# The largest expert moves from the second place to the last, and the final norm runs beside it

## The chip, the core and the metric

The kernel runs on one core of a Trainium2 chip. A core has a matrix engine (PE, with its weight loads shown apart as PEld), a vector engine (DVE), a scalar engine (ACT), GpSimd (POOL) and a synchronisation engine (SP); each works through its own list of instructions in order, and waits on semaphores of the others. 16 DMA engines move data; here SP issues the loads of weights, and POOL the DMAs with indices and those of the final norm. The metric is the time of one execution on the device, in microseconds (us), and the median of several runs is given.

## What is computed

One layer of a hybrid backbone over 1024 latent tokens of 1024 channels: token mixers (spatial gating and bidirectional linear attention), then a mixture of 16 experts of which each token takes two, then a final RMS norm. All values are float32. What matters here is the end:

```python
tokens = (rms_norm(x, g_norm2[layer]) * (1.0 + sc2) + sh2).reshape(-1, d)
...
y = moe_ffn(tokens, w_router, b_router, w_exp_gate[layer], w_exp_up[layer], w_exp_down[layer])
x = x + gt2 * y[:n_lat].reshape(bsz, seq, d)
...
return rms_norm(x, g_final)

def rms_norm(x, g):
    xf = x.astype(jnp.float32)
    y = xf * lax.rsqrt(jnp.mean(xf * xf, axis=-1, keepdims=True) + EPS)
    return (y * g.astype(jnp.float32)).astype(x.dtype)

def expert_block(args):
    xb, e = args
    return (jax.nn.silu(xb @ w_g[e]) * (xb @ w_u[e])) @ w_d[e]
```

With 16 experts and two for each token an expert has 128 tokens on average, some more, some fewer.

## The kernel before

Up to the router the kernel handles mixers and the second norm; the rows after the mixers lie in DRAM as `x1_d`, the normed ones as `h2_d`. Then comes the expert stage, a loop over 16 **slots** (`for e in range(E)`, L1570). `places()` (L1311) ranks the experts by their token counts on the chip, and the table `RANK` (L53) says which rank is worked on in which slot: slot 0 always takes expert 0, slot 1 the rank 1 (the most tokens among the others), slot 15 the rank 15 (the fewest). `UNITS` (L54) follows from it: a slot handles 128 tokens, and besides two, one or no **32-row blocks** for experts with more tokens (two for rank 1, one for ranks 2 to 9, none for the others).

An expert's weights are 18 **pages** of 1 MB: 12 for gate and up (`w_gu`, three thirds of four pages, index `c`), six for down (`w_d`). `load()` (L1175) issues a page on SP into one of ten buffers, in the order of the program, and SP waits there until the buffer is free. Only the 128-row product needs a page split into two parts: `part()` (L1187) makes the high part on ACT (L1192) and the low part on DVE (L1193), into one of three buffers `hl`:

```python
hl = split_tile()
SC.activation(hl[:, 0, :], raw, AF.Copy)
V.tensor_sub(hl[:, 1, :], raw, hl[:, 0, :].bitcast(F32))
```

`block_a` (L1366) multiplies the 128 rows by such a split page, in 12 matmuls of 512 columns. `block_b` (L1376) multiplies the 32-row blocks by the page as it was loaded: the four column quarters of a block stand in the four 32-row strips of the PE's output. In each third a slot with blocks does `block_b` for all four pages first, then `turned_a` (L1557), which transposes the activations of the third before, then `block_a` for the four pages. Behind each third come SiLU on ACT (`sa`, `sb_`) and the product with the up part on DVE. In the down part the pages go in two groups of three, in the same manner. A slot ends with the gate products on DVE, `yb` (L1625) for the blocks and `ya` (L1632) for the 128 rows, and with `put` (L1429): POOL adds the rows into `x1_d` by an indirect DMA that accumulates.

The **final norm** runs beside the last slot. `fetched(i)` (L1507) loads rows 256 i to 256 i + 255 of `x1_d` (block i, 0 to 3) by POOL; it has to wait until the adds of slot 14 have landed. Block 0 has a buffer of its own, the others take page buffers in their turn. `normed(i)` (L1512) squares both halves of the block on ACT (`fq`), makes 1/rms in 12 small steps on DVE (`rstd`, L212), scales by it and by the gain `gf`, and writes to `out` by POOL. `NE` (L48) says for each half who scales: "V" is one DVE operation (L1524), "S" is ACT and then a multiplication on POOL (L1521, L1522). `TAIL` (L49) says behind which third or pair of down pages each step stands in the program (`tail`, L1540). The rows of the last slot's own expert are gathered (`xg`), get `ya` added on the chip, are normed there and scattered over `out` (`put_out`, L1533).

The order on each engine is not that of the program: a scheduler lists each engine's instructions ahead of time, and may put a later step of the program ahead of an earlier one where its data come sooner by its reckoning. If experts overflow their slots, a branch at the end (L1653) repeats work; it is not taken here.

Of the kernel before, what the change touches and what calls it, by code (L numbers as in the profile page):

```python
# [18 lines left out]
S = 1024  # L19
# [25 lines left out]
FQB = 1  # L45
EPX = 1
FOLD = 2
NE = ["SS", "SV", "SV", "VV"]  # L48
TAIL = dict(g0=["f0", "f1"], g2=["g", "n0", "n1", "f2"], d0=["f3"], d2=["n2", "n3"])  # L49
QW = 260  # L50


RANK = (0, 1, 10, 2, 11, 3, 12, 4, 13, 5, 14, 6, 7, 8, 9, 15)  # L53
UNITS = tuple(0 if r == 0 else 2 if r == 1 else 1 if r < 10 else 0 for r in RANK)  # L54
C_C, C_CC, C_G1, C_BB, C_BM, C_GLA, C_LNG = 0, 8, 16, 24, 40, 56, 64
N_COLS = 72
# [105 lines left out]
def body(tc, A, out):  # L162
# [1104 lines left out]
    def pt(name, tag, bufs):  # L1267
        return ps.tile([128, 512], F32, name=name, tag=tag, bufs=bufs)
# [42 lines left out]
    def places():  # L1311

        X = mybir.AxisListType.X
        sq = [128, 16, 16]
        key = ep_.tile([128, 16], F32, name="key")
        V.scalar_tensor_tensor(key, cf, 16.0, ks[:, 3], op0=ALU.mult, op1=ALU.add)
        w = ep_.tile(sq, F32, name="w16")
        V.tensor_tensor(w, key[:, None, :].to_broadcast(sq), key[:, :, None].to_broadcast(sq), op=ALU.is_gt)
        rank = ep_.tile([128, 16], F32, name="rank")
        V.tensor_reduce(rank, w, axis=X, op=ALU.add)  # L1320
        sel = ep_.tile(sq, F32, name="sel")
        V.tensor_tensor(sel, ks[:, 0, :, None].to_broadcast(sq), rank[:, None, :].to_broadcast(sq), op=ALU.is_equal)
        f = ep_.tile([128, 5, 16], F32, name="fi")
        V.tensor_copy(f[:, 0:3], ids)
        V.tensor_scalar(f[:, 3], ks[:, 3], -1.0, 15.0, op0=ALU.mult, op1=ALU.add)
        V.memset(f[:, 3, 0:1], 0.0)
        V.tensor_copy(f[:, 4], cf)
        o = ep_.tile([128, 5, 16], F32, name="fo")
        for i in (3, 0, 1, 2, 4):
            V.tensor_tensor(w, sel, f[:, i, None, :].to_broadcast(sq), op=ALU.mult)  # L1330
            V.tensor_reduce(o[:, i], w, axis=X, op=ALU.add)
            if i == 3:
                V.tensor_mul(key[0:1], o[0:1, 3], ks[0:1, 2])
                V.tensor_reduce(rank[0:1, 0:3], key[0:1, 1:16].rearrange("o (a b) -> o a b", b=5), axis=X, op=ALU.add)
                V.tensor_copy(cnt[:, 0:3], rank[0:1, 0:3])
                words.extend(SP.value_load(cnt[0:1, k:k + 1], min_val=0, max_val=0xFFFFF) for k in range(3))
        V.tensor_copy(ids, o[:, 0:3])
        V.tensor_scalar(tks, ids, 1, None, op0=ALU.logical_shift_right)
        V.tensor_scalar(tkB, tkB, 4, quarter, op0=ALU.mult, op1=ALU.add)
        V.tensor_scalar(chs, ids, 1, None, op0=ALU.bitwise_and)  # L1340

        for b in range(7):
            V.scalar_tensor_tensor(more[:, b], o[0:1, 4], -128.0 * b, ks[0:1, 1], op0=ALU.add, op1=ALU.is_gt)
        V.tensor_copy(more[:, 7], o[0:1, 3])
        V.tensor_copy(more[:, 8], ks[0:1, 1])
        V.tensor_reduce(rank[0:1, 0:1], more[:, 0], axis=X, op=ALU.max)
        V.tensor_copy(cnt[:, 3:4], rank[0:1, 0:1])
# [164 lines left out]
    def normed(i, gf):  # L1512
# [4 lines left out]
            SC.activation(sq, x1[:, j], AF.Square, accum_out=ss[:, 0, j:j + 1])  # L1517
        rstd(ss[:, 1], ss[:, 0], 2, 1.0 / D, ep_)
        for j in range(2):
            if NE[i][j] == "S":  # L1520
                SC.activation(x1[:, j], x1[:, j], AF.Copy, scale=ss[:, 1, j:j + 1])  # L1521
                GP.tensor_mul(x1[:, j], x1[:, j], gf)  # L1522
            else:
                V.scalar_tensor_tensor(x1[:, j], x1[:, j], ss[:, 1, j:j + 1], gf, op0=ALU.mult, op1=ALU.mult)  # L1524
        GP.dma_start(rows_of(out, i), x1)

    def quarters(r0, tile_):
# [10 lines left out]
        return st  # L1538

    def tail(at):  # L1540
        nonlocal gf, xg
        for n in TAIL.get(at, ()):
            if n == "g":
                gf = ep_.tile([128, D], F32, name="gf")
                bcast("rows", 2 * D, D, gf)
                xg = ep_.tile([128, D], F32, name="xg", tag="xa", bufs=1)
                gather(xg, x1_d, tkA[:, E - 1:E])
            elif n[0] == "f":
                fetched(int(n[1]))
            else:  # L1550
                normed(int(n[1]), gf)

    gf = xg = None
    wAB = prep_a(0, *first_xa, ch0), []
    before = []

# [13 lines left out]
    for e in range(E):  # L1570
# [50 lines left out]
        yb = ep_.tile([128, 2, 256], F32, name="yb", bufs=2)  # L1621
        last = e + 1 == E
        wA, wB = wAB_
        for j in range(U):
            V.scalar_tensor_tensor(yb[:, j], pb[:, 256 * j:256 * j + 256], wB[j], g2B, op0=ALU.mult, op1=ALU.mult)  # L1625
        if last:

            sl = ep_.tile([128, 8], F32, name="sl")
            sq = ep_.tile([128, D], BF16, name="fq", bufs=FQB)
        for h in range(2):  # L1630
            hs = slice(512 * h, 512 * h + 512)
            V.scalar_tensor_tensor(ya[:, hs], pa[h], wA, g2A[:, h, :], op0=ALU.mult, op1=ALU.mult)  # L1632
# [3 lines left out]
        if last:  # L1636
            V.tensor_add(sl[:, 6:7], sl[:, 4:5], sl[:, 5:6])
            rstd(sl[:, 7:8], sl[:, 6:7], 1, 1.0 / D, ep_)
            V.scalar_tensor_tensor(xg, xg, sl[:, 7:8], gf, op0=ALU.mult, op1=ALU.mult)
            put_out(xg, tkA[:, e:e + 1], out, S - 1)  # L1640
        if last:
            break
        st = [put(ya, tkA[:, e:e + 1], x1_d, (), before)]
# [9 lines left out]
    any_more = nc.values_load(cnt[0:1, 3:4], min_val=0, max_val=1)  # L1653
    with tc.If(any_more > 0):
        put(ya, tkA[:, E - 1:E], x1_d)
        flat = more.rearrange("o b e -> o (b e)")
        with tc.For_i(0, E, 1) as e:
            with tc.For_i(0, 7, 1) as b:
# [28 lines left out]
```

## Time and profile before

| | |
|---|---|
| time, median of three runs | 2250.44 us (lowest 2249.14 us) |
| the profiled execution: its time | 2251.51 us |
| its span, first to last instruction | 2249.8 us |
| PE busy | 2170.6 us, 96% |
| DVE, ACT, POOL busy | 1415.1, 1056.9, 213.0 us |
| mean granted TensorE clock | 0.984 of 2.4 GHz |

Times of the profile are counted from the start of the span. Lines named L... are those of the kernel before. In a timeline each row is one instruction or a run of like ones; idle time in brackets stands before the row's start. In a table by windows, busy times of PE and PEld overlap. Instructions that only wait or issue a load on SP are not counted as busy.

### The profile page before, as it was taken

To read this page: it belongs to the slowest core of one execution; us is meant where nothing else is said; L and a number is where in the kernel's file an instruction comes from. 1 tells how busy PE (TensorE), PEld (TensorE's weight loads), DVE (VectorE), ACT (ScalarE), POOL (GpSimd) and SP (SyncE) were. 2 spreads that over 40 slices of the span, in tenths; PEclk is the share of its full clock that TensorE was granted. 3 is DMA by queue.
4 is the path that set the end of the run, shared out by engine and by line. 5 is a ranking of instruction groups with operands and counts; after the bars stand their busy time and mean duration, and the time that the engine had idled before them with its cause. 6 is when DMAs were issued, how large, how long until landed. Compare 5 with 4: busy or idle time off the path is not lost. (4 is left out here: it accounts for less than half of the span.)

```text
span 2249.8 us, 36046 instructions
## 1 busy us (share of the span) xinstructions
PE 2170.6 (96%) x14286; PEld 1787.4 (79%) x14287; DVE 1415.1 (63%) x2127; ACT 1056.9 (47%) x1327; POOL 213.0 (9%) x174
## 2 busy tenths in 40 slices
PE   8999999999999999999969999999999999999975
PEld 6999898888889978888967777777778777777754
DVE  5744215847672354245888578787878787677666
ACT  3412114634542244233226456665667576555553
POOL 0011000000000000000342110000101010100031
PEclk9999999999999999999989999999999999999987
DMA  7576433556652176445658779797989898877774
GB/s 295 178 228 177 155 130 102 192 172 208 215 187 71 57 260 208 168 149 195 189 189 319 253 274 362 284 369 297 367 291 377 298 351 314 296 274 284 280 245 157
DMA packets 141792, 529.63 MB, mean 235 GB/s; under 512 B 17127, under 2 KB 57759, under 8 KB 94513
## 3 DMA queue, kind: packets, MB, share of 16 engines
q1 hardware_dynamic: 119584, 467.84, 57.1%
q0 software_dynamic: 20880, 55.16, 8.5%
q10 hardware_dynamic: 1152, 4.26, 0.6%
q8 instruction: 114, 1.87, 0.3%
q14 instruction: 62, 0.50, 0.1%
HBM read 457.09 MB, written 70.31 MB: 234 GB/s over the span
## 5 line engine op out<-in xcount | busy, mean ns | idle before, releaser
L1193 DVE TENSOR_TENSOR hl<-praw,hl 128x2048 fp32r<-128x2048 f32 x174 | 400.2, 2302 | 137.3 <-ACT hl L1192 134.1
L1372 PE MATMUL pa<-hl,xah 128*128 128x512 f32 x1536 | 428.1, 399 | 19.8 <-ACT hl L1192 13.2
L1192 ACT ACTIVATE hl<-praw 128x2048 fp32r<-128x2048 f32 x174 | 333.4, 1918 | 157.8 <-PE pa L1372 150.9
L1372 PEld LDWEIGHTS pa<-hl,xah 128*128 128x128 f32 x1536 | 286.9, 189 | 91.4 <-ACT hl L1192 13.7
L1193 DVE TENSOR_TENSOR hl<-raw,hl 128x2048 fp32r<-128x2048 f32 x114 | 260.7, 2290 | 91.0 <-ACT hl L1192 88.2
L1192 ACT ACTIVATE hl<-raw 128x2048 fp32r<-128x2048 f32 x114 | 218.6, 1918 | 104.0 <-PE pa L1372 98.2
L1372 PE MATMUL pa<-hl,xal 128*128 128x512 f32 x768 | 241.8, 396 | 0.0
L1372 PE MATMUL pa<-hl,aah 128*128 128x512 f32 x768 | 214.8, 401 | 6.3 <-DVE hl L1193 5.0
L256 PE MATMUL mm<-wh,hxh 128*128 128x256 f32 (+1 forms) x768 | 218.2, 284 | 0.9 <-DVE vv L285 0.6
L256 PE MATMUL mm<-wl,hxh 128*128 128x256 f32 (+1 forms) x768 | 216.8, 282 | 0.0
L256 PE MATMUL mm<-wh,hxl 128*128 128x256 f32 (+1 forms) x768 | 216.6, 282 | 0.0
L256 PE MATMUL mm<-hxh,wh 128*128 128x512 f32 x448 | 178.4, 398 | 0.0
L256 PE MATMUL mm<-hxh,wl 128*128 128x512 f32 x448 | 178.2, 398 | 0.0
L256 PE MATMUL mm<-hxl,wh 128*128 128x512 f32 x448 | 178.1, 398 | 0.0
L1372 PEld LDWEIGHTS pa<-hl,xal 128*128 128x128 f32 x768 | 145.5, 189 | 34.0
L1372 PEld LDWEIGHTS pa<-hl,aah 128*128 128x128 f32 x768 | 142.7, 190 | 37.3 <-DVE hl L1193 5.5
L256 PEld LDWEIGHTS mm<-wh,hxh 128*128 128x128 f32 x768 | 144.6, 188 | 1.9 <-DVE vv L285 0.8
L238 DVE TENSOR_TENSOR wl<-wraw,wh 128x2048 fp32r<-128x2048 f32 (+1 forms) x36 | 82.7, 2298 | 99.7 <-ACT wh L237 99.6
L256 PEld LDWEIGHTS mm<-wl,hxh 128*128 128x128 f32 x768 | 144.7, 188 | 0.0
L256 PEld LDWEIGHTS mm<-wh,hxl 128*128 128x128 f32 x768 | 144.4, 188 | 0.0
L1372 PE MATMUL pa<-hl,aal 128*128 128x512 f32 x384 | 121.4, 396 | 0.0
L237 ACT ACTIVATE wh<-wraw 128x2048 fp32r<-128x2048 f32 (+1 forms) x36 | 69.1, 1918 | 67.3 <-PE mm L256 67.0
(489 smaller groups left out, 3588.2 us busy)
## 6 DMA issues: line engine op xcount, KB each, us to landing
praw<-in_w_gu_dram SPq DMA_DIRECT2D x116, 1024.0 KB
raw<-in_w_gu_dram SPq DMA_DIRECT2D x76, 1024.0 KB
praw<-in_w_d_dram SPq DMA_DIRECT2D x58, 1024.0 KB
raw<-in_w_d_dram SPq DMA_DIRECT2D x38, 1024.0 KB
wraw<-in_w_in_dram SPq DMA_DIRECT2D x24, 1024.0 KB
wraw<-in_w_mod_dram SPq DMA_DIRECT2D x18, 1024.0 KB
vb<-v_d POOLq DMA_DIRECT2D x16, 1024.0 KB, 6.3
xt<-in_x_dram SPq DMA_DIRECT2D x16, 512.0 KB
```

The costliest lines, as they stand in the source:

```text
L237: SC.activation(wh[:, :n], raw[:, :n], AF.Copy)
L238: V.tensor_sub(wl[:, :n], raw[:, :n], wh[:, :n].bitcast(F32))
L256: end = PE.matmul(acc, Wst[a](k), Wmv[b](k), start=n == 0, stop=n == tot - 1)
L1192: SC.activation(hl[:, 0, :], raw, AF.Copy)
L1193: V.tensor_sub(hl[:, 1, :], raw, hl[:, 0, :].bitcast(F32))
L1372: end = PE.matmul(acc[h], st[x][:, k0 + k, :], w[:, k, 512 * h:512 * h + 512], start=start and (k, n) == (0, 0), stop=stop and (k, n) == ( ...
```

## The change

The largest expert (rank 1, with its two 32-row blocks) goes from slot 1 to slot 15; the other ranks keep their order, so that slots 1, 3, 5, 7, 9, 11, 13 and 14 have one block, slot 15 has two and the others none. The steps of the final norm move within the last slot (`TAIL`): all four blocks are fetched by the second third, and normed behind the third one and in the down part. All scaling of the norm is done on DVE, none on ACT and POOL. The last expert's 32-row blocks are handled like its 128 rows: their rows of `x1_d` are gathered in quarters (`xq`), `yb` is added, the squares are summed by quarter on ACT, a small matmul with a 0/1 matrix (`k32`) adds the four quarters of each row, DVE makes 1/rms and the product, and POOL scatters the quarters over `out`. For that SP loads the gain in quarters (`gq`, four small DMAs) and `k32`.

```diff
--- before.py
+++ after.py
@@ -45,12 +45,11 @@
 FQB = 1
 EPX = 1
 FOLD = 2
-NE = ["SS", "SV", "SV", "VV"]
-TAIL = dict(g0=["f0", "f1"], g2=["g", "n0", "n1", "f2"], d0=["f3"], d2=["n2", "n3"])
+TAIL = dict(g0=["f0", "f1"], g1=["g", "f2", "f3"], g2=["n0", "n1"], d0=["n2"], d2=["n3"])
 QW = 260
 
 
-RANK = (0, 1, 10, 2, 11, 3, 12, 4, 13, 5, 14, 6, 7, 8, 9, 15)
+RANK = (0, 2, 10, 3, 11, 4, 12, 5, 13, 6, 14, 7, 15, 8, 9, 1)
 UNITS = tuple(0 if r == 0 else 2 if r == 1 else 1 if r < 10 else 0 for r in RANK)
 C_C, C_CC, C_G1, C_BB, C_BM, C_GLA, C_LNG = 0, 8, 16, 24, 40, 56, 64
 N_COLS = 72
@@ -1318,7 +1317,7 @@
         V.tensor_tensor(w, key[:, None, :].to_broadcast(sq), key[:, :, None].to_broadcast(sq), op=ALU.is_gt)
         rank = ep_.tile([128, 16], F32, name="rank")
         V.tensor_reduce(rank, w, axis=X, op=ALU.add)
-        sel = ep_.tile(sq, F32, name="sel")
+        sel = ep_.tile(sq, F32, name="sel", tag="sel")
         V.tensor_tensor(sel, ks[:, 0, :, None].to_broadcast(sq), rank[:, None, :].to_broadcast(sq), op=ALU.is_equal)
         f = ep_.tile([128, 5, 16], F32, name="fi")
         V.tensor_copy(f[:, 0:3], ids)
@@ -1517,11 +1516,7 @@
             SC.activation(sq, x1[:, j], AF.Square, accum_out=ss[:, 0, j:j + 1])
         rstd(ss[:, 1], ss[:, 0], 2, 1.0 / D, ep_)
         for j in range(2):
-            if NE[i][j] == "S":
-                SC.activation(x1[:, j], x1[:, j], AF.Copy, scale=ss[:, 1, j:j + 1])
-                GP.tensor_mul(x1[:, j], x1[:, j], gf)
-            else:
-                V.scalar_tensor_tensor(x1[:, j], x1[:, j], ss[:, 1, j:j + 1], gf, op0=ALU.mult, op1=ALU.mult)
+            V.scalar_tensor_tensor(x1[:, j], x1[:, j], ss[:, 1, j:j + 1], gf, op0=ALU.mult, op1=ALU.mult)
         GP.dma_start(rows_of(out, i), x1)
 
     def quarters(r0, tile_):
@@ -1538,19 +1533,27 @@
         return st
 
     def tail(at):
-        nonlocal gf, xg
+        nonlocal gf, gq, xg, xq, k32
         for n in TAIL.get(at, ()):
             if n == "g":
                 gf = ep_.tile([128, D], F32, name="gf")
                 bcast("rows", 2 * D, D, gf)
                 xg = ep_.tile([128, D], F32, name="xg", tag="xa", bufs=1)
                 gather(xg, x1_d, tkA[:, E - 1:E])
+                gq = ep_.tile([128, 256], F32, name="gq", tag="sel")
+                quarters(2 * D, gq)
+                k32 = ep_.tile([128, 128], F32, name="k32")
+                SP.dma_start(k32, A["k32"])
+                xq = ep_.tile([128, 2, 256], F32, name="xq", tag="xb", bufs=1)
+                for j in range(UNITS[E - 1]):
+                    gather(xq[:, j], x1_quarter, tkB[:, j, E - 1:E])
             elif n[0] == "f":
                 fetched(int(n[1]))
             else:
                 normed(int(n[1]), gf)
 
-    gf = xg = None
+    gf = gq = xg = xq = k32 = None
+    out_quarter = out.rearrange("t (g c) -> (t g) c", g=4)
     wAB = prep_a(0, *first_xa, ch0), []
     before = []
 
@@ -1621,12 +1624,24 @@
         yb = ep_.tile([128, 2, 256], F32, name="yb", bufs=2)
         last = e + 1 == E
         wA, wB = wAB_
+        if last:
+
+            sl = ep_.tile([128, 16], F32, name="sl")
+            sq = ep_.tile([128, D], BF16, name="fq", bufs=FQB)
         for j in range(U):
             V.scalar_tensor_tensor(yb[:, j], pb[:, 256 * j:256 * j + 256], wB[j], g2B, op0=ALU.mult, op1=ALU.mult)
+            if last:
+                V.tensor_add(xq[:, j], xq[:, j], yb[:, j])
+                SC.activation(sq[:, 256 * j:256 * j + 256], xq[:, j], AF.Square, accum_out=sl[:, 8 + j:9 + j])
         if last:
 
-            sl = ep_.tile([128, 8], F32, name="sl")
-            sq = ep_.tile([128, D], BF16, name="fq", bufs=FQB)
+            p = pt("sums", "pt", 2)
+            PE.matmul(p[:, 0:U], k32, sl[:, 8:8 + U], start=True, stop=True)
+            rstd(sl[:, 10:10 + U], p[:, 0:U], U, 1.0 / D, ep_)
+            ends = []
+            for j in range(U):
+                V.scalar_tensor_tensor(xq[:, j], xq[:, j], sl[:, 10 + j:11 + j], gq, op0=ALU.mult, op1=ALU.mult)
+                ends.append(put_out(xq[:, j], tkB[:, j, e:e + 1], out_quarter, 4 * S - 1, ends))
         for h in range(2):
             hs = slice(512 * h, 512 * h + 512)
             V.scalar_tensor_tensor(ya[:, hs], pa[h], wA, g2A[:, h, :], op0=ALU.mult, op1=ALU.mult)
@@ -1637,7 +1652,7 @@
             V.tensor_add(sl[:, 6:7], sl[:, 4:5], sl[:, 5:6])
             rstd(sl[:, 7:8], sl[:, 6:7], 1, 1.0 / D, ep_)
             V.scalar_tensor_tensor(xg, xg, sl[:, 7:8], gf, op0=ALU.mult, op1=ALU.mult)
-            put_out(xg, tkA[:, e:e + 1], out, S - 1)
+            put_out(xg, tkA[:, e:e + 1], out, S - 1, ends)
         if last:
             break
         st = [put(ya, tkA[:, e:e + 1], x1_d, (), before)]
@@ -1653,6 +1668,8 @@
     any_more = nc.values_load(cnt[0:1, 3:4], min_val=0, max_val=1)
     with tc.If(any_more > 0):
         put(ya, tkA[:, E - 1:E], x1_d)
+        for j in range(UNITS[E - 1]):
+            put(yb[:, j], tkB[:, j, E - 1:E], x1_quarter)
         flat = more.rearrange("o b e -> o (b e)")
         with tc.For_i(0, E, 1) as e:
             with tc.For_i(0, 7, 1) as b:
```

Three places of the engines' lists, where the names carry buffer numbers and the lines of the changed kernel stand a few lower or higher than those of the one before. The first is ACT at the start of slot 15. Before, the four pages of the first third end with `hl_18936`; `fq` is the square of block 0 (`fx`), `hl_18968` the split of page 4:

```order
L1192 ACTIVATE hl_18919<-raw_18917 128x2048
L1192 ACTIVATE hl_18936<-raw_18934 128x2048
L1592 ACTIVATE sa_18951<-pa0_18881 128x256
L1592 ACTIVATE sa_18954<-pa1_18882 128x256
L1517 ACTIVATE fq_19134,fs_19135<-fx_18960 128x1024 x2
L1192 ACTIVATE hl_18968<-raw_18966 128x2048
L1521 ACTIVATE fx_18960<-fx_18960,fs_19135 128x1024 x2
L1192 ACTIVATE hl_18992<-praw_18990 128x2048
```

After, `hl_18660` and `hl_18675` are the splits of pages 2 and 3, `sb_` the SiLU of the 32-row blocks of the first third, `fq_19042` the square of block 0, `hl_18799` and `hl_18814` the splits of pages 4 and 5, and `fq_19064` the square of the first half of block 1:

```order
L1191 ACTIVATE hl_18660<-raw_18561 128x2048
L1589 ACTIVATE sb__18690<-pb_18556 128x256
L1191 ACTIVATE hl_18675<-raw_18563 128x2048
L1516 ACTIVATE fq_19042,fs_19043<-fx_18708 128x1024 x2
L1191 ACTIVATE hl_18799<-raw_18715 128x2048
L1516 ACTIVATE fq_19064,fs_19065<-raw_18710 128x1024
L1191 ACTIVATE hl_18814<-praw_18717 128x2048
L1595 ACTIVATE sa_18693<-pa0_18554 128x256
L1595 ACTIVATE sa_18696<-pa1_18555 128x256
```

Block 0's square stands ahead of the split of page 4 in both. The SiLU of the 128 rows of the first third (`sa`) stood ahead of that square and now stands behind it and behind two more splits; ACT's scaling (the row that writes `fx`) is gone.

The second place is DVE in the second third of slot 15. Before, `hl_18968` to `hl_19051` are pages 4 to 8, `aal` the low part of the first third's activations, `rs_` the small steps for block 1:

```order
L1193 TENSOR_TENSOR hl_18968<-raw_18966,hl_18968 128x2048
L1193 TENSOR_TENSOR hl_18992<-praw_18990,hl_18992 128x2048
L1193 TENSOR_TENSOR hl_19009<-praw_19007,hl_19009 128x2048
L1427 TENSOR_TENSOR aal_11408<-aat_18983,aah_11407 128x512
L215 TENSOR_SCALAR rs_m_19162<-fs_19159 128x2
L218 TENSOR_SCALAR rs_t_19165<-rs_m_19162 128x2
L219 TENSOR_SCALAR rs_y_19164<-rs_t_19165 128x2
L1193 TENSOR_TENSOR hl_19026<-praw_19024,hl_19026 128x2048
L221 TENSOR_TENSOR rs_t_19165<-rs_y_19164 128x2
L222 SCALAR_TENSOR_TENSOR rs_t_19165<-rs_t_19165,rs_m_19162 128x2
L223 SCALAR_TENSOR_TENSOR rs_y_19164<-rs_t_19165,rs_y_19164 128x2
L1193 TENSOR_TENSOR hl_19051<-praw_19049,hl_19051 128x2048
```

After, `hl_18844` is page 7 and `hl_18973` page 8; ahead of page 7's split stand both halves of block 1's scaling and the first steps for block 2:

```order
L1426 TENSOR_TENSOR aal_11408<-aat_18788,aah_11407 128x512
L1590 TENSOR_TENSOR sb__18859<-sb__18859,pb_18714 128x256
L222 SCALAR_TENSOR_TENSOR fs_19065<-rs_t_19071,rs_y_19070 128x2
L1519 SCALAR_TENSOR_TENSOR raw_18710<-raw_18710,fs_19065,gf_18868 128x1024 x2
L214 TENSOR_SCALAR rs_m_19189<-fs_19186 128x2
L217 TENSOR_SCALAR rs_t_19192<-rs_m_19189 128x2
L1192 TENSOR_TENSOR hl_18844<-praw_18721,hl_18844 128x2048
L218 TENSOR_SCALAR rs_y_19191<-rs_t_19192 128x2
L220 TENSOR_TENSOR rs_t_19192<-rs_y_19191 128x2
L221 SCALAR_TENSOR_TENSOR rs_t_19192<-rs_t_19192,rs_m_19189 128x2
L222 SCALAR_TENSOR_TENSOR rs_y_19191<-rs_t_19192,rs_y_19191 128x2
L1192 TENSOR_TENSOR hl_18973<-praw_18889,hl_18973 128x2048
```

Before, small steps alone stood between the splits; now whole scalings of 1024 columns stand there too.

The third place is the end of DVE's list, behind the splits of the last pages. Before:

```order
L1193 TENSOR_TENSOR hl_19309<-praw_19307,hl_19309 128x2048
L1193 TENSOR_TENSOR hl_19326<-praw_19324,hl_19326 128x2048
L1632 SCALAR_TENSOR_TENSOR ya_19341<-pa0_19183,wA_18957,g2A_11410 128x512
L1632 SCALAR_TENSOR_TENSOR ya_19341<-pa1_19184,wA_18957,g2A_11410 128x512
L1634 TENSOR_TENSOR xg_19132<-xg_19132,ya_19341 128x512 x2
L1637 TENSOR_TENSOR sl_19343<-sl_19343 128x1
L215 TENSOR_SCALAR rs_m_19352<-sl_19343 128x1
L218 TENSOR_SCALAR rs_t_19355<-rs_m_19352 128x1
L219 TENSOR_SCALAR rs_y_19354<-rs_t_19355 128x1
```

After (`sums` is the output of the small matmul, `xq` the rows of the 32-row blocks):

```order
L1192 TENSOR_TENSOR hl_19328<-praw_19226,hl_19328 128x2048
L1632 SCALAR_TENSOR_TENSOR yb_19344<-pb_19088,wB0_18702,g2B_11412 128x256
L1632 SCALAR_TENSOR_TENSOR yb_19344<-pb_19088,wB1_18705,g2B_11412 128x256
L1634 TENSOR_TENSOR xq_18879<-xq_18879,yb_19344 128x256 x2
L1647 SCALAR_TENSOR_TENSOR ya_19343<-pa0_19086,wA_18699,g2A_11410 128x512
L214 TENSOR_SCALAR rs_m_19355<-sums_19353 128x2
L1649 TENSOR_TENSOR xg_18870<-xg_18870,ya_19343 128x512
L217 TENSOR_SCALAR rs_t_19358<-rs_m_19355 128x2
L1647 SCALAR_TENSOR_TENSOR ya_19343<-pa1_19087,wA_18699,g2A_11410 128x512
L218 TENSOR_SCALAR rs_y_19357<-rs_t_19358 128x2
L1649 TENSOR_TENSOR xg_18870<-xg_18870,ya_19343 128x512
L220 TENSOR_TENSOR rs_t_19358<-rs_y_19357 128x2
```

The work on the 32-row blocks stands ahead of `ya`, and the steps of their 1/rms are interleaved with the work on the 128 rows.

## Rows read from the trace of the kernel before

**Rows 1.** The page: the span, and the line of its part 1 (for each engine busy us, share of the span, instructions).

```profile
span 2249.8 us, 36046 instructions
...
PE 2170.6 (96%) x14286; PEld 1787.4 (79%) x14287; DVE 1415.1 (63%) x2127; ACT 1056.9 (47%) x1327; POOL 213.0 (9%) x174
```

**Rows 2.** Busy time by windows, one window for each of six slots. A window runs from the first gate product of one slot (DVE, L1632) to that of the next: slots 1, 2, 3, 12, 14 and 15. Columns: start and end in us, length, then for each engine its busy us and recorded instructions, the granted TensorE clock (1.00 is 2.4 GHz, 0.50 is 1.2 GHz), the busy share of the DMA engines, GB/s.

```profile
1243.30:1329.20 85.90, 85.90 (x807) 61.96 (x796) 50.44 (x43) 40.91 (x36) 10.10 (x5) 1.00 0.71 249
1329.20:1381.80 52.60, 52.60 (x264) 42.17 (x267) 47.65 (x35) 38.96 (x31) 5.81 (x2) 1.00 0.97 372
1381.80:1451.40 69.60, 69.60 (x511) 51.93 (x504) 48.92 (x41) 40.40 (x36) 6.77 (x4) 1.00 0.82 297
...
2010.30:2080.30 70.00, 69.98 (x533) 51.45 (x529) 48.91 (x40) 40.73 (x37) 6.96 (x4) 1.00 0.80 290
2080.30:2149.90 69.60, 69.60 (x511) 51.93 (x504) 48.95 (x41) 40.39 (x36) 5.96 (x3) 1.00 0.78 281
2149.90:2232.00 82.10, 57.31 (x222) 43.68 (x220) 58.45 (x83) 44.95 (x45) 23.52 (x14) 0.83 0.63 225
```

**Rows 3.** Waits of the PE in the window of slot 15: engine, line and tile that waited, what it waited for, us in total, times, longest.

```profile
PE pa L1372 <- ACT hl L1192: 14.5, 2, 13.2
...
PE pa L1372 <- DVE hl L1193: 10.2, 5, 5.0
```

**Rows 4.** Timeline at the start of slot 15. Columns: start in us, length in us, engine, line, operation, out<-in, count, and in brackets the idle time before it with what ended it.

```profile
2148.04 0.87 PEld L1372 LDWEIGHTS pa<-hl,xah 128*128 128x128 f32 x4
...
2149.89 1.40 DVE L1632 SCALAR_TENSOR_TENSOR ya<-pa,wA,g2A 128x512 f32<-128x512 f32 x2
...
2151.57 3.36 POOL L1430 DMA_INDIRECT x_d<-ya,tks  x1 [7.49 <-DVE ya L1632]
...
2163.20 0.81 POOL L1510 DMA_DIRECT2D fx<-x_d  x1 [8.28 <-DMA x_d<-ya,tks]
...
2168.57 1.06 ACT L1517 ACTIVATE fq<-fx 128x1024 bf16<-128x1024 f32 x1 [8.57 <-DMA fx<-x_d]
...
2170.81 1.89 ACT L1192 ACTIVATE hl<-raw 128x2048 fp32r<-128x2048 f32 x1
2170.93 0.17 DVE L215 TENSOR_SCALAR rs_m<-fs 128x2 f32<-128x2 f32 x1 [10.11 <-ACT fq L1517]
...
2172.76 1.22 PE L1372 MATMUL pa<-hl,xah 128*128 128x512 f32 x2 [13.21 <-ACT hl L1192]
```

**Rows 5.** Busy time by windows inside slot 15: two pauses of the PE, and the stretch behind each. Columns as in Rows 2.

```profile
2158.90:2172.75 13.85, 0.65 (x3) 0.19 (x1) 2.54 (x14) 4.75 (x7) 2.60 (x3) 0.63 0.65 222
2172.75:2179.60 6.85, 5.28 (x12) 3.69 (x13) 4.93 (x5) 6.29 (x6) 5.05 (x2) 0.50 0.40 146
...
2211.75:2216.80 5.05, 0.02 (x1) 0.00 (x0) 4.88 (x9) 3.40 (x2) 0.76 (x1) 0.70 1.01 341
2216.80:2220.60 3.80, 3.79 (x9) 3.02 (x10) 3.80 (x2) 0.00 (x0) 0.00 (x0) 0.51 0.77 309
```

**Rows 6.** Groups by line in the window of slot 15, different shapes apart: line, engine, operation, out<-in, shapes, count | busy us, mean ns of one | idle time before.

```profile
L1193 DVE TENSOR_TENSOR hl<-raw,hl 128x2048 fp32r<-128x2048 f32 x6 | 13.6, 2285 | 0.0
...
L1192 ACT ACTIVATE hl<-praw 128x2048 fp32r<-128x2048 f32 x10 | 18.9, 1906 | 8.1 <-DVE hl L1193 6.0 <-PE pa L1372 2.0
...
L1427 DVE TENSOR_TENSOR aal<-aat,aah 128x512 fp32r<-128x512 f32 x3 | 2.0, 679 | 0.0
...
L1593 DVE TENSOR_TENSOR sa<-sa,pa 128x256 f32<-128x256 f32 x6 | 2.2, 417 | 5.2 <-ACT sa L1592 5.2
...
L1524 DVE SCALAR_TENSOR_TENSOR praw<-praw,fs,gf 128x1024 f32<-128x1024 f32 x2 | 2.6, 1282 | 0.0
...
L1522 POOL TENSOR_TENSOR fx<-fx,gf 128x1024 f32<-128x1024 f32 x2 | 7.6, 3807 | 8.4 <-ACT fx L1521 8.4
```

**Rows 7.** Timeline in slot 15: a split on DVE, the output DMA of block 1 that POOL issues at the same moment, and the next page load that SP issues. Columns as in Rows 4.

```profile
2197.36 2.27 DVE L1193 TENSOR_TENSOR hl<-praw,hl 128x2048 fp32r<-128x2048 f32 x1
2197.41 0.76 POOL L1525 DMA_DIRECT2D out_dram<-raw  x1 [1.66 <-DVE raw L1524]
...
2202.04 0.34 SPq L1179 DMA_DIRECT2D raw<-in_w_d_dram  x1
```

**Rows 8.** Timeline behind the last matmul. Columns as in Rows 4.

```profile
2231.96 1.41 DVE L1632 SCALAR_TENSOR_TENSOR ya<-pa,wA,g2A 128x512 f32<-128x512 f32 x2 [3.86 <-PE pa L1372]
2233.28 1.28 DVE L1634 TENSOR_TENSOR xg<-xg,ya 128x512 f32<-128x512 f32 x2
...
2235.37 0.16 DVE L1637 TENSOR_TENSOR sl<-sl 128x1 f32<-128x1 f32 x1 [0.80 <-ACT fq L1635]
...
2237.68 0.16 DVE L223 SCALAR_TENSOR_TENSOR sl<-rs_t,rs_y 128x1 f32<-128x1 f32 x1
2237.88 1.28 DVE L1639 SCALAR_TENSOR_TENSOR xg<-xg,sl,gf 128x1024 f32<-128x1024 f32 x1
2239.45 1.05 POOL L1534 DMA_INDIRECT out_dram<-xg,tks  x1 [16.08 <-DVEq L1654]
```

**Rows 9.** Groups by line from slot 2 to slot 14: the gate product of a 32-row block. Columns as in Rows 6.

```profile
L1625 DVE SCALAR_TENSOR_TENSOR yb<-pb,wB,g2B 128x256 f32<-128x256 f32 x8 | 3.8, 476 | 0.0
```

**Rows 10.** All DMAs of line L1510 (the fetches of the final norm, 1 MB each): time from issue to landing.

```profile
DMA to landing us min/median/max: 5.4/6.5/7.7
```

**Rows 11.** All DMAs of tile `ya` (the adds of 128 rows into x1, L1430): time from issue to landing.

```profile
DMA to landing us min/median/max: 11.7/12.3/13.4
```

## Prediction, written before the changed kernel ran

> **What bounds the kernel now.** I read the page first. The PE is busy for 96% of the span and nothing else comes near [rows 1], so outside a few places time is PE work. To find those places I cut the expert stage into windows from the first gate product (`ya`, L1632) of one slot to that of the next [rows 2]. In slots 1, 2, 3, 12 and 14 the PE is busy to the last tenth of a microsecond, at granted clock 1.00. The length follows the number of 32-row blocks alone: 52.6 us with none (52.5 us used below), 69.6 us with one (70.0 us where the next slot has a block too), 85.9 us with two. The exception is slot 15: no block, yet 82.1 us with the PE busy for 57.3 us at clock 0.83 [rows 2]. So some 29.6 us go into waits there, and that is what this change can reach.
>
> The waits of the PE name the cause: 14.5 us for ACT's half of a page split, of which 13.2 us at once, and 10.2 us for DVE's half [rows 3]. The timeline shows the chain [rows 4]. G stands below for the first gate product of slot 14 (2149.89), from which all times in slot 15 count. The last add into `x1` is issued at G+1.7, the fetch of block 0 waits for it until G+13.3, and its square starts on ACT at G+18.7. That square stands ahead of the split of page 4 (the first order rows of the change), so ACT idles for 8.57 us and the PE for 13.21 us. Behind pauses the clock falls: after this one the next 6.85 us run at 0.50, after the 5.05 us pause at 2211.75 the next 3.8 us at 0.51 [rows 5].
>
> **The change, term by term.**
>
> *Slots 1 to 14.* They lose the two-block slot and get a one-block slot: the 85.9 us go, while one more 52.5 us slot without a block comes in among them and the neighbours keep their lengths. After: six slots of 69.6, six of 52.5 and two of 70.0 (slots 13 and 14, whose successors have blocks) make 872.6 us. Before, the windows ran from 1243.3 to 2149.9, 906.6 us [rows 2]. Term: **-33.9 to -34.0 us**. It is PE work that moves to the end; nothing is saved by this alone.
>
> *Last slot, without waits.* A page costs 52.5/18 = 2.92 us for the 128 rows, and (85.9-52.5)/18 = 1.86 us for two blocks [rows 2]. 18 pages of both make 86.0 us; the PE starts them 1.9 us ahead of G (2148.04, [rows 4]), so 84.1 us from G.
>
> *What covers block 0's fetch now.* The 32-row product runs on unsplit pages, and the code puts it first in each third. So the PE has 7.4 (pages 0 to 3, blocks), 11.7 (the same, 128 rows) and 7.4 us (pages 4 to 7, blocks) ahead of it before anything behind the square is needed: until G+24.6. The square would start at G+18.7 as before. The add's landing is 11.7 us at least and 13.4 us at most [rows 11], and slot 15's was a fast one; the fetch took 5.4 us, others up to 7.7 us [rows 10]. So G+18.7 to G+22.7; one page load now shares the DMA engines with it, and I take **G+20.0**.
>
> *Then DVE is the bound, not ACT.* The order puts all normalisation on DVE between the splits. From the square's start to the `sa` products: 2.36 us until the first small step [rows 4], 11 small steps of 0.195 (2235.37 to 2237.68 for 12, [rows 8]), split of page 4 2.29, one step, one half of block 0 1.28, two `sa` 0.83 [rows 6]: 9.1 us. So G+29.1, while the PE is free at G+24.6: **wait of 4.5 us**. From there to the end of page 7's split: six small copies 1.2, two splits 4.57, the other half of block 0 1.28, 10 small steps 1.95, `aal` 0.68, `sb_` 0.5 (bounded by `sa` 0.42 and `aal` 0.68), a step 0.2, both halves of block 1 2.56, two steps 0.4 and page 7's split 2.29 (the second DVE order rows): 15.6 us, so G+44.7. The PE gets through pages 4 to 6 by G+37.9 at full clock: **wait of up to 6.8 us**; whatever the lower clock takes after the first wait comes off this one. After it, page 7 2.9 us, plus **1.9 us** for 3.8 us at half clock [rows 5].
>
> *Rest of the slot.* Ten pages of each kind, 47.8 us. I find no wait in it: DVE's split of page 11, behind blocks 2 and 3, is done about 1 us ahead of the PE. Page 12's buffer is block 1's, so SP's loads of pages 12 to 17 stand behind that output. The output would be issued near G+42 and SP goes on 4.6 us later [rows 7], while the PE wants page 12 near G+68. If that cover were gone, each us would count. Sum: 44.7+2.9+1.9+47.8 = 97.3 us against 82.1: **+15.2 us**.
>
> *POOL and SP.* POOL loses four multiplications of up to 3.8 us [rows 6]; none is on the new chain. It gains two gathers, and all four fetches now stand in a row. SP gets five small loads, put among slot 2's pages: 0.34 us each of issue [rows 7], hidden while SP waits for buffers; 0 to 1.7 us, I take 0. The Trainium skill, page "SBUF — State Buffer", section "SBUF: two separate sides", warns that POOL cannot write DMA descriptors while certain DVE operations hold a shared port. By that rule, each fetch here could wait out a 2.3 us DVE operation. Against it, POOL's DMA at 2197.41 took 0.76 us inside a 2.27 us split [rows 7].
>
> *Behind the last matmul.* Before, from the gate product to the last product's end: 2231.96 to 2239.16, 7.2 us [rows 8]. New on DVE there (third order rows): 12 small steps of the blocks' own rstd, 2.3 us, and two 256-column products, 0.476 each [rows 9]; they fill the 0.80 us in which DVE waited for ACT [rows 8]. Term: **+2.5 us** (1.5 if more gaps fill, 3.3 if none). The blocks' gate products and adds (4 x 0.48) run while the PE does the last page; uncovered they cost 1.9. The `k32` matmul of two columns lies between nothing and a twelfth of a page, 0.24 us, beside `ya`. The two extra scatters (1.05 us each by [rows 8]) are issued while DVE works on the last 128 rows; uncovered, 2.1.
>
> *Sum.* -33.9 +15.2 +2.5 = -16.2 us. The profiled execution took 2251.5 us (span 2249.8 us): 2235.3 us. It lies 1.1 us above the median, 2250.4 us, so **2234 us**.
>
> **The rivals.** *All of it hides* (13%): the PE never waits in the last slot. For it: G+24.6 against G+20.0. Against it: DVE's order. 84.1 in place of 97.3: 2221 us.
>
> *More waits* (20%): blocks 2 and 3, whose squares stand in ACT's order ahead of splits, land late, or the clock stays low for three more pages, as it did for 6.85 us at 2172.75 [rows 5]. Three pages at half speed add 8.7 us: 2243 us.
>
> *Loads too slow early* (7%): slot 1 now leaves 16.3 us less to fill the page buffers, and slot 2 draws 372 GB/s at a DMA share of 0.97 [rows 2]. Against it: slot 1 has share 0.71. 16.3 us at the 123 GB/s between them is 2 MB, 5.4 us: 2240 us.
>
> *Slower* (5%): block 0's square gates DVE, so each us that it starts later is a us. If it starts after G+36.2, 16.2 us later than taken, the change loses; 20 us later gives 2254 us. Against it: the slowest add and fetch together make 4 us.
>
> **How the numbers follow.** My forecast has 55%, its own range 2229 to 2240 us. The range 2222 to 2246 us leaves out about 6% below (full hiding) and 12% above (the worst of more waits, and slower). Two per cent, about what a measurement of this kernel can tell, is 45 us: more than the whole 29.6 us. So faster 1%, same 97%, slower 2%.
>
> **What would show it.** Right: the gate product of slot 14 near 2116; the PE's first wait in slot 15 shortly behind 32-row work, not 13 us; a second at page 7 for DVE; a last window near 97 us; 9.7 us from the last gate products to the last product. Wrong: a window near 84 or above 105; PE waits in slots 2 to 4; a page load that waits for an output while the PE waits for that page.

## The result and the profile after

The changed kernel takes 2235.63 us (median of 7 runs, 2231.19 to 2240.86) against 2249.80 us for the kernel before (median of 6): the ratio is put at 0.9929, with a 95% interval from 0.9915 to 0.9944. Measured again beside the last four experiments it took 2237.26 against 2251.79 us, 0.9930 (0.9913 to 0.9946). Two runs of the kernel before that took over 3 ms are left out, as disturbed, of the ratios and of the medians given here and below (with them the medians are 2250.44 and, beside the first four experiments, 2252.12 us). The forecast was 2234 us. The gain, 0.6 to 0.9% by the interval, is less than the two per cent from which the prediction speaks of faster, as it had said. The profiled execution took 2239.81 us. The page of it, with the lines that answer to [rows 1]:

```profile
span 2238.0 us, 36086 instructions
...
PE 2169.4 (97%) x14288; PEld 1788.1 (80%) x14289; DVE 1417.0 (63%) x2147; ACT 1052.8 (47%) x1327; POOL 204.2 (9%) x172
```

The windows from gate product to gate product, as in [rows 2], for slots 1, 2, 12, 14 and 15 (the gate product `ya` now stands in L1647):

```profile
1248.60:1318.20 69.60, 69.60 (x511) 51.92 (x504) 48.92 (x41) 40.39 (x36) 6.99 (x4) 1.00 0.85 308
1318.20:1370.70 52.50, 52.50 (x260) 42.08 (x262) 47.55 (x35) 38.79 (x31) 5.84 (x2) 1.00 0.97 372
...
1928.70:1981.20 52.50, 52.50 (x260) 42.12 (x262) 47.55 (x34) 38.80 (x31) 5.81 (x2) 1.00 0.97 372
...
2051.30:2121.50 70.20, 70.18 (x532) 51.73 (x528) 48.89 (x40) 40.89 (x37) 7.92 (x5) 1.00 0.74 261
2121.50:2218.80 97.30, 88.31 (x797) 62.90 (x786) 60.90 (x98) 43.46 (x51) 16.46 (x12) 0.95 0.57 209
```

Slot 1 is 69.6 us long in place of 85.9, and slot 15 97.3 in place of 82.1. Slot 12 takes 52.5 in place of 70.0, since rank 15, which has no block, now stands there, ahead of ranks 8 and 9 (the section on the change says that the other ranks keep their order; rank 15 does not). The other slots keep their lengths within 0.7 us. (In [rows 2] the fourth row is that of slot 13, not 12; both took 70.0.) The two profiled executions divide as follows (us, from the first instruction's start):

| | before | after | difference | predicted |
|---|---|---|---|---|
| up to slot 0's gate product | 1243.35 | 1248.58 | +5.2 | 0 |
| slots 1 to 14 | 906.54 | 872.96 | -33.6 | -33.9 |
| slot 15 | 82.08 | 97.25 | +15.2 | +15.2 |
| last `ya` to the end of the last product | 7.20 | 8.25 | +1.05 | +2.5 |
| from there to the end | 10.61 | 10.97 | +0.4 | 0 |
| span | 2249.8 | 2238.0 | -11.8 | -16.2 |

The first line is work that the change doesn't touch. In the ten profiled executions of this study it lies between 1240.6 and 1248.6 us, without order by kernel: two kernels with the changed order of experts have 1240.6 and 1243.5. It puts this profile 4 us above its median. That the runs spread over 10 us may come from it too, but no trace shows that, and what causes it was not looked into.

The waits of PE in slot 15, which answer to [rows 3]:

```profile
PE aat L1565 <- DVE sa L1596: 6.6, 1, 6.6
PE pa L1371 <- DVE hl L1192: 2.3, 1, 2.3
PE pa L1371 <- ACT hl L1191: 0.2, 1, 0.2
```

Of 24.7 us of waits about 9 are left. The timeline shows whence (G is now 2121.53; L1516 is the square, L1519 the scaling, L1191 and L1192 the two halves of a split, L1595 and L1596 make `sa`):

```profile
2121.53 1.41 DVE L1647 SCALAR_TENSOR_TENSOR ya<-pa,wA,g2A 128x512 f32<-128x512 f32 x2
...
2123.22 3.37 POOL L1429 DMA_INDIRECT x_d<-ya,tks  x1 [8.11 <-DVE ya L1647]
...
2135.84 0.81 POOL L1509 DMA_DIRECT2D fx<-x_d  x1 [9.25 <-DMA x_d<-ya,tks]
...
2144.06 1.06 ACT L1516 ACTIVATE fq<-fx 128x1024 bf16<-128x1024 f32 x1 [11.74 <-DMA fx<-x_d]
...
2146.29 1.89 ACT L1191 ACTIVATE hl<-raw 128x2048 fp32r<-128x2048 f32 x1
...
2148.48 2.29 DVE L1192 TENSOR_TENSOR hl<-raw,hl 128x2048 fp32r<-128x2048 f32 x1
...
2150.69 0.15 DVE L222 SCALAR_TENSOR_TENSOR fs<-rs_t,rs_y 128x2 f32<-128x2 f32 x1
2150.88 1.28 DVE L1519 SCALAR_TENSOR_TENSOR fx<-fx,fs,gf 128x1024 f32<-128x1024 f32 x1
...
2152.08 0.74 DVE L1596 TENSOR_TENSOR sa<-sa,pa 128x256 f32<-128x256 f32 x2
...
2152.55 1.12 PE L1565 MATMUL aat<-kf,sa 128*128 128x128 f32 x4 [6.56 <-DVE sa L1596]
...
2162.11 2.48 DVE L1519 SCALAR_TENSOR_TENSOR raw<-raw,fs,gf 128x1024 f32<-128x1024 f32 x2
...
2164.78 2.29 DVE L1192 TENSOR_TENSOR hl<-praw,hl 128x2048 fp32r<-128x2048 f32 x1
2164.89 0.74 POOL L1520 DMA_DIRECT2D out_dram<-raw  x1 [2.88 <-DVE rs_t L217]
...
2167.13 0.90 PE L1371 MATMUL pa<-hl,xah 128*128 128x512 f32 x2 [2.26 <-DVE hl L1192]
```

The reader is to see a chain of single files. The square of block 0 starts at G+22.5, 8.2 us after its fetch was issued. DVE then makes 1/rms, with the split of page 4 in between (its last step but one ends at 2148.56, its last starts at 2150.69), scales half a block, and only then makes the `sa` products, for whose transposition (`aat`) PE has waited 6.56 us. The second wait ends with page 7's split, ahead of which DVE scaled block 1 for 2.48 us. Four windows show the clock behind these waits:

```profile
2152.55:2157.20 4.65, 4.65 (x14) 3.94 (x15) 4.65 (x9) 1.85 (x2) 3.79 (x1) 0.50 0.50 203
2157.20:2164.00 6.80, 6.76 (x29) 5.08 (x28) 6.42 (x18) 4.94 (x8) 4.20 (x4) 0.99 0.58 193
2167.50:2170.90 3.40, 3.40 (x10) 2.66 (x9) 3.37 (x12) 2.97 (x4) 0.00 (x0) 0.50 0.42 159
2170.90:2218.00 47.10, 47.10 (x453) 33.49 (x452) 30.95 (x34) 19.46 (x21) 1.41 (x2) 1.00 0.46 180
```

It stands at 0.50 (1.2 GHz) behind each, and from 2170.9 on PE is busy without a gap at 1.00. The tail, which answers to [rows 8]:

```profile
2218.79 0.75 DVE L1647 SCALAR_TENSOR_TENSOR ya<-pa,wA,g2A 128x512 f32<-128x512 f32 x1 [6.74 <-PE pa L1371]
...
2222.02 0.16 DVE L222 SCALAR_TENSOR_TENSOR rs_y<-rs_t,rs_y 128x2 f32<-128x2 f32 x1
2222.22 0.16 DVE L220 TENSOR_TENSOR rs_t<-rs_y 128x2 f32<-128x2 f32 x1
...
2222.41 0.16 DVE L221 SCALAR_TENSOR_TENSOR rs_t<-rs_t,rs_m 128x2 f32<-128x2 f32 x1
2222.51 0.16 DVE L1652 TENSOR_TENSOR sl<-sl 128x1 f32<-128x1 f32 x1
2222.61 0.16 DVE L222 SCALAR_TENSOR_TENSOR rs_y<-rs_t,rs_y 128x2 f32<-128x2 f32 x1
2222.70 0.15 DVE L214 TENSOR_SCALAR rs_m<-sl 128x1 f32<-128x1 f32 x1
...
2225.75 1.28 DVE L1654 SCALAR_TENSOR_TENSOR xg<-xg,sl,gf 128x1024 f32<-128x1024 f32 x1
```

### The profile page after: what moved, and what is told of

The parts are those of the page before. It is cut to its first block, busy times and chain, and to the rows that moved or that the text cites. A ratio compares the mean times of both kernels' runs of the same rounds, so it can differ in the third digit from the quotient of the medians.

```text
span 2238.0 us, 36086 instructions
## 1 busy us (share of the span) xinstructions
PE 2169.4 (97%) x14288; PEld 1788.1 (80%) x14289; DVE 1417.0 (63%) x2147; ACT 1052.8 (47%) x1327; POOL 204.2 (9%) x172
## 5 line engine op out<-in xcount | busy, mean ns | idle before, releaser
L1192 DVE TENSOR_TENSOR hl<-praw,hl 128x2048 fp32r<-128x2048 f32 x173 | 395.8, 2291 | 127.6 <-ACT hl L1191 123.3
L1191 ACT ACTIVATE hl<-praw 128x2048 fp32r<-128x2048 f32 x173 | 331.7, 1918 | 149.3 <-PE pa L1371 149.3
L1192 DVE TENSOR_TENSOR hl<-raw,hl 128x2048 fp32r<-128x2048 f32 x115 | 263.1, 2290 | 89.5 <-ACT hl L1191 79.2
L1191 ACT ACTIVATE hl<-raw 128x2048 fp32r<-128x2048 f32 x115 | 220.6, 1918 | 106.8 <-PE pa L1371 101.9
```

## The experiments

There were eight runs, the last of them the change itself. The first four were measured beside 13 undisturbed runs of the kernel before (median 2251.44 us), the last four beside another 7 (2251.79 us).

**The order of the experts alone.** The change with `TAIL`, `NE` and the norm's scaling as before:

```diff
-TAIL = dict(g0=["f0", "f1"], g1=["g", "f2", "f3"], g2=["n0", "n1"], d0=["n2"], d2=["n3"])
+NE = ["SS", "SV", "SV", "VV"]
+TAIL = dict(g0=["f0", "f1"], g2=["g", "n0", "n1", "f2"], d0=["f3"], d2=["n2", "n3"])
...
```

> The ranks and the in-place norm of the last expert's 32-row blocks as in the change, but the four-block norm placed and divided over ACT, POOL and DVE as before. Theory (the 32-row product covers the fetch of block 0, and DVE's list is what is left of the wait): the wait ahead of the first transposes stays at 5 to 6.5 us, because block 0's square still stands ahead of the splits of pages 4 and 5; the wait at page 7 goes, because block 0 is scaled on ACT and POOL and only one half of block 1 stands on DVE ahead of page 7's split. Last window 90 to 93 us against 97.3 with the whole change, time 2227 to 2232 us. Rival (the new placement of the norm, all on DVE, is what hides it): without it the last window is as long over its pure work as before, 84 + 30 = 114 us, time about 2252 us.

Measured: 2243.06 us (4 runs), 0.9956 (0.9939 to 0.9972); slot 15 takes 102.9 us. The first wait stayed at 6.5 us and the second shrank to 1.0, but a third of 6.32 us appeared at G+64. Both sizes expected were missed: the window lies between that of the theory and that of the rival. Its timeline ahead of that wait:

```profile
2181.83 0.16 DVE L215 TENSOR_SCALAR rs_m<-fs 128x2 f32<-128x2 f32 x1
...
2181.86 2.41 POOL L1522 TENSOR_TENSOR raw<-raw,gf 128x1024 f32<-128x1024 f32 x1 [13.16 <-ACT raw L1521]
...
2182.03 2.27 DVE L218 TENSOR_SCALAR rs_t<-rs_m 128x2 int32<-128x2 int32 x1
...
2186.98 2.48 DVE L1524 SCALAR_TENSOR_TENSOR praw<-praw,fs,gf 128x1024 f32<-128x1024 f32 x2
2189.38 6.69 DVE L1193 TENSOR_TENSOR hl<-raw,hl 128x2048 fp32r<-128x2048 f32 x3
...
2191.72 1.22 PE L1372 MATMUL pa<-hl,xah 128*128 128x512 f32 x2 [6.32 <-DVE hl L1193]
```

A step over 128x2 elements, of a kind that takes 0.16 to 0.17 us elsewhere, takes 2.27 us here, for as long as POOL multiplies (2181.86 to 2184.27). Behind it stand both blocks' chains and scalings, and only then the splits for which PE waits. The Trainium skill, page "SBUF — State Buffer", section "SBUF: two separate sides", says that GpSimd and some DVE operations share a pair of ports as an exclusive lock, and the one that comes second waits for the other's whole instruction. This row agrees with it.

**The norm's placement alone.** The kernel before with `TAIL` of the change and all scaling on DVE:

> The ranks as before (last slot without 32-row blocks), the four-block norm placed as in the change and all on DVE. Theory: nothing covers the fetch of block 0, and four fetches in a row make it land later; the PE waits 13 to 17 us there and again for DVE; last window 80 to 88 us against 82.1 before, time 2248 to 2256 us. Rival (the placement hides the norm): last window 55 to 70 us, time 2223 to 2238 us.

Measured: 2254.4 us (10 runs), 1.0014 (1.0004 to 1.0024); slot 15 takes 81.8 us against 82.1. Its waits of PE in slot 15 are nearly those of [rows 3]:

```profile
PE pa L1371 <- ACT hl L1191: 17.0, 2, 14.6
PE pa L1371 <- DVE hl L1192: 8.0, 6, 2.9
```

What the change does to the norm gains nothing in the old order; by the interval it costs a little.

**Block 1 fetched first.** The change with `g0=["f1", "f0"]`:

> The change with the fetch of block 1 issued ahead of that of block 0; the square of block 0 then stands behind the split of page 4, still ahead of that of page 5. Theory (the PE's first wait follows from the landing of the block whose square stands in ACT's list, the second from the sum of DVE's list): block 0's square starts about 2.5 us later than at G+22.5, the first wait is 6 to 8 us, the second 2 to 5 us, last window 96 to 99 us. Rival (ACT's order alone sets the wait, so one split more ahead of the square takes it away): first wait under 3 us, last window under 94 us.

Measured: 2235.26 us (1 run); slot 15 takes 97.8 us.

```profile
2131.32 0.81 POOL L1509 DMA_DIRECT2D raw<-x_d  x1 [9.65 <-PE pa L1371]
...
2132.11 0.79 POOL L1509 DMA_DIRECT2D fx<-x_d  x1
...
2142.54 1.06 ACT L1516 ACTIVATE fq<-fx 128x1024 bf16<-128x1024 f32 x1 [12.39 <-DMA fx<-x_d]
...
2148.20 1.11 PE L1565 MATMUL aat<-kf,sa 128*128 128x128 f32 x4 [7.17 <-DVE sa L1596]
```

Block 0's square starts at G+25.9 in place of 22.5, the first wait is 7.17 us in place of 6.56, the second 1.85, a little under what was expected. The square of block 0 feeds the first wait, but ACT's order changed too: a split and `sa` went ahead of what stood behind the square, so 3.4 us more cost only 0.5 us in all (one run).

**Squares held behind splits.** The change, with each block's square made to wait for ACT's split of page 6, 7, 9 or 11 of the last slot, so that it can't stand ahead of a split whose page has landed:

```diff
+HOLD = (6, 7, 9, 11)
...
+    splits = []
...
-            SC.activation(hl[:, 0, :], raw, AF.Copy)
+            splits.append(SC.activation(hl[:, 0, :], raw, AF.Copy))
...
-            SC.activation(sq, x1[:, j], AF.Square, accum_out=ss[:, 0, j:j + 1])
+            s = SC.activation(sq, x1[:, j], AF.Square, accum_out=ss[:, 0, j:j + 1])
+            tc.add_manual_dep(s.ins, splits[18 * (E - 1) + HOLD[i]].ins.name, SYNC, reason="behind the split")
```

> The change, with the squares of blocks 0, 1, 2 and 3 held behind ACT's halves of the splits of pages 6, 7, 9 and 11 of the last slot; the same work otherwise. Theory (the order of squares and scalings between the splits is all that is left of the PE's waits): no wait of the PE over 2 us in pages 4 to 11; page 12 may come up to 3 us late since its load stands behind block 1's output; last window 84 to 88 us, time 2221 to 2227 us. Rival (DVE has too much work in the last slot, in whatever order): the waits come back elsewhere, last window 94 us or more.

Measured: 2224.89 us (4 runs, 2218.1 to 2227.77), 0.9884 (0.9867 to 0.99): the fastest kernel of this study. The window of slot 15 and, from the timeline, ACT around block 0's square (G is 2113.50; L1193 is ACT's split, L1598 makes `sa`):

```profile
2113.50:2197.30 83.80, 83.80 (x793) 60.13 (x786) 60.98 (x97) 43.78 (x51) 14.28 (x12) 1.00 0.66 243
```

```profile
2130.44 0.66 ACT L1598 ACTIVATE sa<-pa 128x256 f32<-128x256 f32 x2 [0.64 <-PE pa L1373]
...
2130.98 1.91 ACT L1193 ACTIVATE hl<-praw 128x2048 fp32r<-128x2048 f32 x1
...
2135.93 1.06 ACT L1518 ACTIVATE fq<-fx 128x1024 bf16<-128x1024 f32 x1 [3.04 <-DMA fx<-x_d]
```

PE is busy for all 83.8 us at clock 1.00. The square starts at G+22.4, as in the change, but the splits of pages 4 to 6 and `sa` are done by then. DVE is busy for 60.98 us, as long as in the change (60.90), so the amount of its work is not the limit either. Not the late fetch but what stood behind it made the waits.

**The old order, held as well.** The kernel before with the change's norm, its squares held behind pages 9, 11, 12 and 14:

> The kernel before (largest expert second) with the final norm placed and computed as in the change, and each block's square held behind ScalarE's split of page 9, 11, 12 or 14 of the last slot, so that no square stands ahead of a split whose page has landed. It asks how much of the gain of the held version is due to the order of the experts at all. Theory: the 32-row work moves no time by itself, it only fills time that the last slot would otherwise wait or spend on VectorE. Held, the last window of the old order has 52.5 us of products and VectorE busy for 57.6, so VectorE becomes the bound: a window of 60 to 66 us instead of 81.8, no wait of TensorE over 3 us, 2233 to 2240 us; the changed order held stays ahead by 8 to 16 us, since its 83.8 hide VectorE's 61 entirely. Rival: without the 32-row products nothing covers the fetches and rows' chain at all; the waits only move to later pages, the window is 75 to 82 us, 2247 to 2254 us.

Measured: 2239.28 us (4 runs), 0.9941 (0.9924 to 0.9957). The window of slot 15:

```profile
2151.10:2218.90 67.80, 57.26 (x222) 44.12 (x220) 56.87 (x86) 40.22 (x41) 11.26 (x9) 0.90 0.75 280
```

67.8 us in place of 81.8, a little above what was expected: DVE is busy for 56.9, but waits of up to 3.8 us remain. With the norm of the change, which alone gains nothing, holding the squares gains 12.5 us without moving any expert, nearly as much as the change; both together gain 26.6. The held new order stays some 14 us ahead. The two were held behind different pages, and no other choice of pages was run.

**The order alone, all scaling on DVE.** The first experiment with every half in `NE` set to "V":

> The order of the experts alone, with the norm's fetches and blocks placed as before, but all eight halves scaled by VectorE alone (no ScalarE scaling, no POOL product). The run with the order alone had a wait of 6.3 us at G + 64, in which a VectorE step of 128x2 took 2.27 us beside a POOL product of 2.41 us and two blocks' chains stood ahead of a split. Theory: that wait comes from the split of the halves over three engines; here it is under 2 us, the last window is 96 to 99 us and the first wait still 6.5. Rival: it comes from where blocks 2 and 3 are placed; it stays at 4 us or more and the window is 101 us or more.

Measured: 2239.87 us (2 runs), 0.9945 (0.9925 to 0.9965); slot 15 takes 101.3 us.

```profile
PE pa L1372 <- DVE hl L1193: 6.1, 2, 3.1
PE aat L1570 <- DVE sa L1601: 5.0, 1, 5.0
```

No step of DVE is drawn out here. The third wait is 3.1 us, in between the two expectations, and the window is the rival's. So about half of the 6.3 us of that wait came from the split over three engines, and the other half goes with where blocks 2 and 3 stand. The window gains less, 1.6 us. The second wait grew from 1.0 to 3.0 us, as both halves of block 1 are scaled on DVE ahead of that split again. The waits fell by 3.3 us in all, but the clock stands at 0.50 behind the longer second wait too, and PE is busy for 90.2 us of the window in place of 88.5.

**The tail's two chains apart.** The change, with the 128 rows' 1/rms (L1652 to L1653) listed behind the 32-row blocks' last product:

> The change, with the 128 rows' inverse root put behind the 32-row blocks' last product on VectorE instead of between their steps. Theory: a step that needs the one before it starts 0.195 us after it, and a step of the other chain fits between for nothing, so the 32-row chain ends no earlier and the twelve steps of the 128 rows (0.195 each, 2.3 us) come behind it: the last product over xg ends 0.8 to 1.0 us later, 9.1 us after the last gate product's start instead of 8.25. Rival: steps cost their time either way, the interleaving saves nothing, and the last product ends within 0.2 us of where it does in the change.

Measured: 2238.68 us (1 run). The last `ya` starts at 2216.76:

```profile
2222.24 0.16 DVE L1653 TENSOR_TENSOR sl<-sl 128x1 f32<-128x1 f32 x1
2222.44 0.15 DVE L214 TENSOR_SCALAR rs_m<-sl 128x1 f32<-128x1 f32 x1
2222.63 0.15 DVE L217 TENSOR_SCALAR rs_t<-rs_m 128x1 int32<-128x1 int32 x1
...
2224.77 1.29 DVE L1655 SCALAR_TENSOR_TENSOR xg<-xg,sl,gf 128x1024 f32<-128x1024 f32 x1
```

The steps now follow each other at 0.19 to 0.20 us, and the last product ends 9.30 us after the last `ya` in place of 8.25: 1.05 us later, close to what was expected. Interleaving did save that.

**The change once more.**

> The change itself once more, beside the others on one chip: slots 1 to 14 873.0, last window 97.3 with a first wait of 6.5 us and a second of 2 to 4; 2231 to 2241 us, the spread coming from before slot 0 ends.

Measured: 2237.26 us (4 runs); slots 1 to 14 872.95, slot 15 97.0 with waits of 6.3 and 2.3 us.

## Why the prediction was right

The forecast of 2234 us lies 1.6 us from the median. One account puts all kernels that ran more than once in their order, and within 3.5 us of their gains. Slot 15 needs 84.1 us of PE work in the new order (the prediction's figure; the held kernel took 83.84 without a wait). That figure leaves out the 1.9 us by which PE starts ahead of G. For the old order the prediction took 52.5 us without leaving them out; by one count it is 50.6, and the kernel before lost 31.5 us in slot 15, not 29.6. The work there grows by 33.5 us, which is what slots 1 to 14 give up (33.6). So the gain should be 31.5 less what a kernel loses (its window less its work), and less 1.4 us behind the last `ya` where the largest expert is last.

| kernel | window | lost | gain so worked out | gain measured |
|---|---|---|---|---|
| the change | 97.25 | 13.15 | 17.0 | 14.2 and 14.5 |
| order alone | 102.92 | 18.8 | 11.3 | 8.4 |
| order alone, DVE scales | 101.31 | 17.2 | 12.9 | 11.9 |
| norm alone | 81.76 | 31.2 | 0.3 | -3.0 |
| old order, held | 67.88 | 17.3 | 14.2 | 12.5 |
| change, held | 83.84 | 0 | 30.1 | 26.6 |

The account gives too much every time, by 1.0 to 3.5 us. It rests on stages of single profiles, and leaves out the line ahead of slot 0, the only other one that differs by so much; where the excess comes from stays open.

So the prediction's mechanism stands: moving PE work gains nothing, and having it where the last slot would wait does. What remains is set, as it said, by the single file behind block 0's square. But it named DVE as the bound, and the held kernel shows that DVE's work would have fitted: the order of squares, scalings and splits makes the waits. By its steps:

- *Slots 1 to 14*: -33.6 for -33.9.
- *The cover*: 32-row work was to last until G+24.6; PE's wait began at G+24.46.
- *Block 0's square*: taken at G+20.0 within 18.7 to 22.7, it was at 22.5. The fetch was issued 1.0 us later than before (G+14.3 for 13.3) and took 2.8 us longer. The prediction named the four fetches that now stand in a row, but put only one page load into the price. With four in a row, block 0's fetch took 6.4 to 8.2 us from issue to square (the change twice, the held one, the tails apart), with two, 5.3 to 5.6 us (the kernel before, both runs with the order alone, the norm alone). But in the old order, held, it took 7.0 us to its landing with two in a row, so the number in a row is not shown to be the cause.
- *"Each us that it starts later is a us"* (the rival "Slower"): true of the first wait, not of the window. With the tails apart the square stood 1.2 us earlier than in the change (G+21.4), the first wait was 1.2 us shorter (5.4), and the window only 0.4 (96.87); with block 1 fetched first it stood 3.4 us later for 0.5.
- *First wait*: 6.56 for 4.5, since the square was 2.5 us late; the chain from it to the end of the `sa` products was 8.8 us for 9.1.
- *Second wait*: page 7's split was done at G+45.5 for 44.7 (six copies took 0.65 us, not 1.2, and the chain 23.0 us for 24.7, which offset the late square). PE waited 2.3 us of the "up to 6.8": the first wait was longer, and 4.65 us at half clock cost 2.3, which the prediction had said would come off.
- *Clock behind the second wait*: 3.4 us at 0.50 cost 1.7 for 1.9. 9.0 us of waits and 4.0 of clock make 13.0 of the 13.15 lost.
- *Rest of the slot*: no wait, as said, and no loss in slots 2 to 4 (52.5 for slot 2).
- *Tail*: the term of the sum that was furthest off, +1.05 for +2.5. It priced 12 steps of the blocks' chain at 0.195 each as if DVE were taken by them. The steps of one chain fit into the gaps of the other, and much of the rest lay beside the `ya` products and ACT.
- *POOL's DMAs beside DVE*: no stall is seen after the change either; at 2164.89 a DMA took 0.74 us inside a split of 2.29. The prediction had read the rule of the Trainium skill (page "SBUF — State Buffer", section "SBUF: two separate sides") too widely: that section counts operations of two tensors, as a split is, among those that were not seen to stall a DMA. The trace agrees.

That the window came out at 97.25 for 97.3 is in part luck: two errors cancel (a later square, a shorter chain). So is part of the 1.6 us: from slot 1 on the profiles gain 17.0 us for the forecast's 16.2, and the medians 14.2. Of the signs, the gate product of slot 14 was to be near 2116 and came at 2121.5, nearly all of it by the 5.2 us ahead of slot 0. The rival that all of it hides was one dependency for each square away: the held kernel is that case, at 2224.9 for 2221.

## What to carry to other kernels

Look at what stands behind a waiting instruction on an in-order engine before moving work to fill the wait: holding back the squares of each block, with the norm's new placement, gained almost as much as moving an expert, and both together nearly twice as much. Heavy work in the last slot pays by what it hides, so work out the loss there (window less matrix work), not the work that moves.

## What the runs showed of the hardware

- On DVE a small step (128x1 or 128x2) starts 0.195 us after the one whose result it needs (2222.02, 2222.22, 2222.41 in the tail), but two chains interleave at 0.08 to 0.11 us a step (2222.41, .51, .61, .70), though each row says 0.15 to 0.16 us. Taking the chains apart cost 1.05 us.
- A 128x2 step on DVE took 2.27 us beside a POOL multiplication of 2.41 that had started 0.17 us ahead of it (order alone).
- Four fetches in a row on POOL are issued 0.7 to 0.8 us apart, and the first took 6.4 to 8.2 us until its square. With one other right behind it, it took 5.3 to 5.6 us in four kernels, and 7.0 to its landing in the old order, held; what makes the difference was not singled out.
